# The inverse of the next head pair and half of its chain operands, made between the chunks of the present chain

## The chip, the cores and the metric

One Trainium2 chip, one core. The metric is the device time of one execution in microseconds, as the median of the runs; beside it stands one execution that the hardware profiler recorded, and every row below is from that one.

## The reference, cut to what matters

One block of a streaming encoder over 1024 tokens of width 1024. A combined projection feeds two groups: sparse attention, whose indexer picks the keys of every query, and RWKV-7 time mixing. Both results go through an output projection and then an MLP of width 4096.

```
step(state, inp):                      # RWKV-7, one token, 8 heads of 64
    r_t, w_t, k_t, v_t, kk_t, a_t = inp
    sa = einsum('bhij,bhj->bhi', state, -kk_t)
    state = (state * w_t[:, :, None, :] + sa[..., None] * (kk_t * a_t)[:, :, None, :]
             + v_t[..., None] * k_t[:, :, None, :])
    return state, einsum('bhij,bhj->bhi', state, r_t)
_, out = lax.scan(step, state0, xs)

h = RMSNorm(x) * (1 + sc1) + sh1 ;  proj = h @ w_in  ->  p_a (attention), p_b (RWKV)
x = x + gt1 * (concat(dsa_attention(p_a), rwkv7_time_mix(p_b)) @ w_out)
u = relu((RMSNorm(x) * (1 + sc2) + sh2) @ w_ff1) ;  x = x + gt2 * ((u * u) @ w_ff2)
```

## The kernel before, in words

The tokens are worked in two halves (hf 0 and 1) of 512. The order in which the code is written is: projections of half 0, RWKV of half 0, attention projections of half 0, indexer of half 0, RWKV projections of half 1, attention of half 0, RWKV of half 1, attention projections of half 1, output projection and MLP of half 0 (with indexer and attention of half 1 hung into it), MLP of half 1. A tile scheduler turns that order into one fixed queue for each engine: what is written earlier has priority, what is not ready by the scheduler's own reckoning lets later work go first. So the large projection matmuls (`dense`, tile ps_mm, with the operands hh, hl, whi, wlo) fill the places between the small matmuls of RWKV and of the indexer. Each engine then works its queue strictly in the written order.

RWKV runs over 4 pairs of heads (j = 0 to 3), and each pair over 8 chunks of 64 tokens:

- `rwkv_feat`: decays, keys and the lower-triangular products Lb and KR of a pair; it ends with BKs on POOL.
- `rwkv_feat2`: the other operands of the chain: Mt (the product `ps_c<-KR,wrec`, masked on DVE), the transposed values (`ps_c<-con,v`, copied by ACT into UV and Vbd) and BKn (`ps_c<-con,BKs`, copied by ACT).
- `rwkv_inv`: the inverse of the chunks' unit-triangular matrices, into TT: 15 pairs of a DVE multiplication (ytmp) and a DVE subtraction (Y), two DVE transposes (D, AT), then four groups of 32x32 matmuls, AT·Lc, D·Gs, AT·Lb, D·Gs, with an ACT copy or a DVE step between them.
- `rwkv_chain`: the recurrence. A chunk is `ps_o<-Vbd,Mt` and `ps_o<-H,KR` on PE, Xb on DVE, `ps_c<-Xb,TT` on PE, UV on DVE and Ub on ACT, `ps_c<-UV,BKn` and `ps_o<-Ub,Lb` on PE, the state H on DVE and On on ACT. The next chunk needs H.
- `rwkv_out`: the normalised output of a pair, written back to memory.

`rwkv` writes, for each j: feat2(j), the whole chain(j), out(j-1), the inverse of j+1, feat(j+2). PSUM has two buffers each for the tags mm, f and c and one each for dx and o; chain, feat2 and inverse all share the two buffers of c.

Of the kernel before, what the change touches and what calls it, by code (L numbers as in the profile page):

```python
# [111 lines left out]
def body(tc, I, out, dbg=None):  # L112
# [475 lines left out]

    def rwkv_feat2(hf, j, R, gp):
        mark('feat%d%d' % (hf, j))  # L590
        R["Mt"] = Mt = gp.tile([128, 8, 2, 64], F32, name="Mt", tag="Mt", bufs=1)
        R["BKn"] = BKn = gp.tile([128, 8, 128], F32, name="BKn", tag="BKn", bufs=1)
        R["UV"] = UV = gp.tile([128, 8, 128], F32, name="UV", tag="UV", bufs=1)
        gram(R["Kh"], R["KR"], Mt, "c")

        pn = pst("c")
        for c in range(4):
            T.transpose(pn[:, c * 128:c * 128 + 128], R["v2"][:, 2 * c:2 * c + 2, :].rearrange("p a b -> p (a b)"), ident)
        pn3 = pn.rearrange("p (a b) -> p a b", a=4)
        for e in range(2):  # L600
            q = slice(e * 64, e * 64 + 64)
            A.copy(UV[64:128].rearrange("p (a e) b -> p a e b", e=2)[:, :, e, :], pn3[q])
            for h in range(2):
                r = slice(h * 64, h * 64 + 64)
                A.copy(R["Vbd"][r].rearrange("p (a e) h b -> p a e h b", e=2)[:, :, e, h, :],
                       pn3[q, :, h * 64:h * 64 + 64])
        for u in (0, 4):
            pn = pst("c")
            for c in range(4):
                T.transpose(pn[:, c * 128:c * 128 + 128], flat(R["BKs"][:, u + c, :, :]), ident)  # L610
            A.copy(BKn[:, u:u + 4, :], pn.rearrange("p (a b) -> p a b", a=4))

    def rwkv_inv(hf, j, R, rp):
# [21 lines left out]
        for c in range(15, 0, -1):  # L635
            t0 = c // 4
# [5 lines left out]
            V.tensor_tensor(y, y, tv, ALU.subtract)  # L642
        D = rp.tile([128, 8, 32], F32, name="D", tag="D", bufs=1)
# [4 lines left out]
        pg, pf = pst("c"), pst("c")  # L648
# [18 lines left out]
        pg = pst("c")  # L667
# [9 lines left out]
        pf = pst("c")  # L677
# [9 lines left out]
    def rwkv_chain(hf, j, R, rp):  # L687
# [3 lines left out]
        On = rp.tile([128, 4, 2, 64], F32, name="On", tag="On", bufs=2)  # L691
        for c in range(8):
# [21 lines left out]
        return On  # L714
# [428 lines left out]
    def rwkv_head(hf, rp):  # L1143
# [182 lines left out]
```

## Time and profile before

| what | value |
|---|---|
| median of 3 runs | 1786.07 us (1786.06 to 1786.14) |
| the profiled execution | 1783.31 us, its span 1781.5 us, mean granted TensorE clock 0.971 |
| PE busy | 1613.9 us, 91% of the span |
| DVE, ACT, POOL busy | 1060.6, 871.5, 557.7 us |

A busy time is the union of an engine's recorded spans; idle time is the rest of the window. A row of the waits says which instruction ended an engine's idle time. The rows themselves stand in the section below.

### The profile page before, as it was taken

How to read it: one execution, taken by the hardware profiler on the slowest of the kernel's cores; microseconds unless marked ns; L12 is line 12 of the kernel's file. 1: busy time of each engine (PE TensorE's matmuls, PEld its weight loads, DVE VectorE, ACT ScalarE, POOL GpSimd, SP SyncE). 2: the span in 40 equal slices, each digit the busy share in tenths (PEclk: the TensorE clock that was granted, in tenths of full speed). 3: DMA queues.
4: the chain of work that ended last, by engine and by line, in shares of the span. 5: the costliest groups of instructions: out<-in, count | busy, mean ns of one | idle time of the engine just before them, and what ended most of it. 6: DMA issues, size and time to landing. Idle time of an engine off the chain costs nothing. (4 is left out here: it accounts for less than half of the span.)

```text
span 1781.5 us, 27231 instructions
## 1 busy us (share of the span) xinstructions
PE 1613.9 (91%) x9380; PEld 1208.7 (68%) x9380; DVE 1060.6 (60%) x2701; ACT 871.5 (49%) x1792; POOL 557.7 (31%) x751
## 2 busy tenths in 40 slices
PE   6997888998778888997968999999999999999998
PEld 3785656666555665674646666777886788888887
DVE  4777677639877777646999558863114233333333
ACT  3324454545547545435845864775235252525251
POOL 3556334443440243433224464113554300000000
PEclk9998999999899999998979999999999999999999
DMA  9885226234343543212112234324332433333332
GB/s 311 281 294 170 81 79 194 84 101 134 101 119 128 156 137 101 61 53 68 41 50 75 71 96 125 84 84 146 103 96 70 122 110 96 98 95 95 96 99 72
DMA packets 264016, 203.89 MB, mean 114 GB/s; under 512 B 17299, under 2 KB 218003, under 8 KB 263878
## 3 DMA queue, kind: packets, MB, share of 16 engines
q1 hardware_dynamic: 253122, 182.90, 34.2%
q10 hardware_dynamic: 10628, 19.24, 2.9%
q8 instruction: 74, 1.21, 0.3%
q14 instruction: 64, 0.52, 0.1%
q0 software_dynamic: 128, 0.01, 0.0%
HBM read 173.32 MB, written 28.78 MB: 113 GB/s over the span
## 5 line engine op out<-in xcount | busy, mean ns | idle before, releaser
L136 POOL TENSOR_TENSOR wlo<-wraw,whi 128x256 fp32r<-128x256 f32 x512 | 400.6, 805 | 658.1 <-ACT whi L394 589.9
L121 PE MATMUL ps_mm<-hh,whi 128*128 128x512 f32 (+1 forms) x1024 | 419.1, 410 | 22.1 <-DVE acca L930 4.1
L394 ACT CAST whi<-wraw 128x512 fp32r<-128x512 f32 x384 | 235.7, 616 | 408.3 <-PE ps_mm L121 378.0
L121 PE MATMUL ps_mm<-hl,whi 128*128 128x512 f32 (+1 forms) x1024 | 417.5, 408 | 2.8 <-DVE hl L384 1.8
L121 PE MATMUL ps_mm<-hh,wlo 128*128 128x512 f32 (+1 forms) x1024 | 418.2, 408 | 0.4
L121 PEld LDWEIGHTS ps_mm<-hh,whi 128*128 128x128 f32 (+1 forms) x1024 | 196.0, 192 | 68.8 <-issue 9.1
L121 PEld LDWEIGHTS ps_mm<-hh,wlo 128*128 128x128 f32 (+1 forms) x1024 | 196.2, 192 | 46.0 <-issue 7.4
L121 PEld LDWEIGHTS ps_mm<-hl,whi 128*128 128x128 f32 (+1 forms) x1024 | 196.3, 192 | 44.3 <-issue 4.8
L121 PE MATMUL ps_mm<-uh,whi 128*128 128x512 f32 x512 | 205.1, 401 | 17.3 <-ACT whi L394 5.7
L121 PE MATMUL ps_mm<-ul,whi 128*128 128x512 f32 x512 | 204.7, 400 | 6.0 <-DVE ul L1118 6.0
L121 PE MATMUL ps_mm<-uh,wlo 128*128 128x512 f32 x512 | 204.4, 399 | 0.8 <-POOL wlo L136 0.5
L396 DVE TENSOR_TENSOR wlo<-wraw,whi 128x512 fp32r<-128x512 f32 x128 | 88.2, 689 | 130.3 <-ACT whi L394 130.3
L915 ACT ACTIVATE jka<-sc,canda 128x1024 bf16<-128x1024 f32 (+1 forms) x93 | 90.1, 969 | 82.5 <-DVE canda L913 57.3
L121 PEld LDWEIGHTS ps_mm<-uh,whi 128*128 128x128 f32 x512 | 97.7, 191 | 44.0 <-ACT whi L394 8.6
L121 PEld LDWEIGHTS ps_mm<-ul,whi 128*128 128x128 f32 x512 | 97.7, 191 | 29.8 <-DVE ul L1118 8.3
L121 PEld LDWEIGHTS ps_mm<-uh,wlo 128*128 128x128 f32 x512 | 97.9, 191 | 24.7 <-POOL wlo L136 2.5
L1124 DVE SCALAR_TENSOR_TENSOR xT<-ps_mm,mod,xT 128x512 f32<-128x512 f32 x64 | 47.9, 748 | 110.7 <-PE ps_mm L121 110.6
L1118 DVE TENSOR_TENSOR ul<-ur,uh 128x512 fp32r<-128x512 f32 x64 | 44.3, 692 | 80.6 <-ACT uh L1117 80.5
L1023 DVE CUSTOM_DVE_ANT_0 L<-ps_f,mk 128x512 f32<-128x512 f32 (+3 forms) x96 | 51.8, 554 | 31.5 <-PE ps_f L121 16.4
L705 ACT COPY Ub<-ps_c 64x64 f32<-64x64 f32 x128 | 26.3, 206 | 72.8 <-DVE UV L703 68.7
L1029 ACT ACTIVATE L<-L,m 128x128 f32<-128x128 f32 (+7 forms) x64 | 49.6, 776 | 18.6 <-DVE m L1026 14.2
L1042 ACT COPY PT<-ps_c 128x512 f32<-128x512 f32 (+3 forms) x96 | 42.5, 479 | 28.8 <-PE ps_c L1041 25.8
(329 smaller groups left out, 2601.4 us busy)
## 6 DMA issues: line engine op xcount, KB each, us to landing
wraw<-in_w_ff_dram SPq DMA_DIRECT2D x256, 256.0 KB, 2.6
wraw<-in_w_in_dram SPq DMA_DIRECT2D x92, 256.0 KB, 3.3
mraw<-in_w_ada_dram SPq DMA_DIRECT2D x64, 256.0 KB, 4.6
mraw<-in_w_ada_dram SPq DMA_DIRECT2D x16, 512.0 KB, 10.7
wraw<-in_w_out_dram SPq DMA_DIRECT2D x32, 256.0 KB, 2.6
rkvd<-shy ACTq DMA_DIRECT2D x24, 256.0 KB
xin<-in_x_dram SPq DMA_DIRECT2D x8, 512.0 KB, 6.5
rt<-rnd SPq DMA_DIRECT2D x32, 128.0 KB, 3.1
```

Of the source, the lines that this page charges most:

```text
L121: r = T.matmul(out, lhsT, rhs, start=start, stop=stop, **kw)
L136: G.tensor_tensor(o[:, c], a[:, c], b[:, c], op)
L394: (A.copy if HE[GRP[0]] == "a" else V.tensor_copy)(hi[:, :, 0:M], raw[:, :, 0:M])
L396: (V if LE[GRP[0]] == "v" or LE[GRP[0]] == "m" and GRP[1] else InHalves).tensor_tensor(lo[:, :, 0:M], raw[:, :, 0:M], hi[:, :, 0:M].bitcas ...
L705: (V.tensor_copy if CE[2] == "v" else A.copy)(Ub[h * 64:h * 64 + 64, h, :], pu[u, h * 64:h * 64 + 64])
L915: A.activation(jka[:, 0:width(b)], sc[b], AF.Sign, scale=-1.0, bias=0.0 if bit == 31 else canda.bitcast(F32)[:, i:i + 1], accum_out=ca[:, ...
L1023: V.tensor_tensor_reduce(L[:, c0:c0 + n], ps[:, 0:n], masks[b][:, c0:c0 + n], 1.0, -3e38, ALU.add, ALU.max, m2[:, pc:pc + 1])
L1029: A.activation(L[:, 0:W], L[:, 0:W], AF.Exp, bias=m2[:, 2:3], accum_out=m2[:, 3:4])
L1042: (A.copy if ((pc + h) % 2 if PTE == 0 else h if PTE == 1 else PTE == 2) else V.tensor_copy)(pT[:, c0:c0 + n], px[:, 0:n])
L1118: V.tensor_tensor(b, r, a.bitcast(F32), ALU.subtract)
L1124: V.scalar_tensor_tensor(xT[:, d, :], ps, mod[:, 40 + d:41 + d], xT[:, d, :], ALU.mult, ALU.add)
```

## The change

`rwkv_inv` becomes a generator that stops before each of its 15 steps and before its transposes, takes PSUM of tag f where it took c, and orders each of its DVE multiplications behind the last H update that has been written. `rwkv_feat2` makes four chunks at a time (u = 0 or 4), with Mt, BKn and UV in tiles that stay for all pairs. `rwkv_chain` becomes a generator that stops after every chunk. `rwkv` then writes for each j: chunk 0, one step of the inverse of j+1, out(j-1); after each later chunk three more steps; after chunk 4 the first half of feat2(j+1); after chunk 7 the rest of the inverse, the second half of feat2(j+1) and feat(j+2). For pair 0 both halves of feat2 stand ahead of feat(1). No arithmetic is added or left out: the transposes of v, and the ACT copies of them, are made in two pieces each.

```diff
-    def rwkv_feat2(hf, j, R, gp):
+    def rwkv_feat2(hf, j, R, u):
-        gram(R["Kh"], R["KR"], Mt, "c")
+        gram(R["Kh"], R["KR"], R["Mt"], "c", (u,))
...
-    def rwkv_inv(hf, j, R, rp):
+    def rwkv_inv(hf, j, R, rp, tag="f"):
...
         for c in range(15, 0, -1):
+            yield
...
-            V.tensor_tensor(tv, L2[:, :, c * 32:c * 32 + c].unsqueeze(3).to_broadcast([128, 2, c, n]),
+            r = V.tensor_tensor(tv, L2[:, :, c * 32:c * 32 + c].unsqueeze(3).to_broadcast([128, 2, c, n]),
                             Y2[:, :, c * 8 + t0:c * 8 + 4].unsqueeze(2).to_broadcast([128, 2, c, n]), ALU.mult)
+            order(r, chained[0])
...
-        pg, pf = pst("c"), pst("c")
+        pg, pf = pst(tag), pst(tag)
...
-                V.scalar_tensor_tensor(H[r, h, :], H[r, h, :], WC[r, c:c + 1], ph[r, h * 64:h * 64 + 64],
-                                       ALU.mult, ALU.add)
+                chained[0] = V.scalar_tensor_tensor(H[r, h, :], H[r, h, :], WC[r, c:c + 1], ph[r, h * 64:h * 64 + 64],
+                                                    ALU.mult, ALU.add)
...
+        setup(0)
+        for u in (0, 4):
+            rwkv_feat2(hf, 0, R[0], u)
         R[1] = rwkv_feat(hf, 1, L4, rp, bp)
         for j in range(4):
...
-            rwkv_feat2(hf, j, R[j], bp)
-            On[j] = rwkv_chain(hf, j, R[j], bp)
-            for w in OR:
-                if w == "o" and j > 0:
-                    rwkv_out(hf, j - 1, R[j - 1], On[j - 1], sg, bp)
-                if w == "i" and j < 3:
-                    rwkv_inv(hf, j + 1, R[j + 1], rp)
-                if w == "f" and j < 2:
-                    R[j + 2] = rwkv_feat(hf, j + 2, L4, rp, bp)
+            for c in rwkv_chain(hf, j, R[j], On[j]):
+                for _ in range(1 if c == 0 else 3):
+                    next(inv, None)
+                if c == 0 and j > 0:
+                    rwkv_out(hf, j - 1, R[j - 1], On[j - 1], sg, bp)
+                if c == 4 and j < 3:
+                    rwkv_feat2(hf, j + 1, R[j + 1], 0)
+            for _ in inv:
+                pass
+            if j < 3:
+                rwkv_feat2(hf, j + 1, R[j + 1], 4)
+            if j < 2:
+                R[j + 2] = rwkv_feat(hf, j + 2, L4, rp, bp)
```

In PE's queue of the kernel before, this is what stands between the last matmul of chain 0 in half 0 and the first of chain 1 (`ps_o<-Vbd,Mt`); two stretches are left out between the pieces.

```order
L121 MATMUL ps_o<-Ub_1569,Lb 128x128
L121 MATMUL ps_c<-AT,Lc 32x32 x32
L121 MATMUL ps_f<-KR,Bh 64x128 x3
L121 MATMUL ps_c<-D,Gs 32x32 x32
L121 MATMUL ps_f<-KR,Bh 64x128 x5
...
L121 MATMUL ps_c<-AT,Lb 32x32 x16
...
L598 MATMUL ps_c<-con,v_1579 128x128 x4
L121 MATMUL ps_f<-w2a,tw 128x128 x3
L121 MATMUL ps_dx<-asq,con 128x512
L610 MATMUL ps_c<-con,BKs 128x128 x4
L121 MATMUL ps_o<-Vbd,Mt 128x128
```

In the changed kernel the same queue, from the same matmul of chain 0 to the first one of chain 1, has only the second half of feat2 and two products of the next feat.

```order
L121 MATMUL ps_o<-Ub_1569,Lb 128x128
L121 MATMUL ps_c<-KR,wrec 64x128 x8
L598 MATMUL ps_c<-con,v_1632 128x128 x2
L121 MATMUL ps_f<-w2a,tw 128x128 x4
L121 MATMUL ps_f<-xa,a2w 128x512
L609 MATMUL ps_c<-con,BKs 128x128 x4
L121 MATMUL ps_o<-Vbd,Mt 128x128
L121 MATMUL ps_o<-H_120,KR 128x128
```

The matmuls of the inverse have moved up, ahead of the last two chunks of chain 0: this is chunk 6 to chunk 7 of chain 0 in the changed kernel, where `ps_f<-AT,Lc` and `ps_f<-D,Gs` stand ahead of the chunk's own `ps_c<-UV,BKn` and `ps_c<-Xb,TT`.

```order
L121 MATMUL ps_c<-Xb_1567,TT_1310 128x128
L121 MATMUL ps_f<-AT,Lc 32x32 x14
L121 MATMUL ps_c<-UV,BKn 128x128
L121 MATMUL ps_f<-AT,Lc 32x32 x3
L121 MATMUL ps_o<-Ub_1569,Lb 128x128
L121 MATMUL ps_f<-AT,Lc 32x32 x15
L121 MATMUL ps_o<-Vbd,Mt 128x128
L121 MATMUL ps_o<-H_119,KR 128x128
L121 MATMUL ps_mm<-hl,whi 128x512
L121 MATMUL ps_f<-D,Gs 32x32 x32
L121 MATMUL ps_c<-Xb_1567,TT_1310 128x128
```

Counted in PE's queue, the number of ps_mm matmuls that stand ahead of a place is, before and after the change:

| place in PE's queue | before | after |
|---|---|---|
| half 0: first matmul of chain 0, 1, 2, 3 | 420, 481, 533, 615 | 385, 482, 518, 588 |
| half 0: last matmul (`ps_o<-Ub,Lb`) of chain 0, 1, 2, 3 | 476, 524, 599, 680 | 482, 518, 588, 640 |
| first and last score matmul (kiH, iqs) of the indexer of half 0 | 743, 787 | 694, 736 |
| first `ps_f<-w2a,tw` of half 1 | 944 | 944 |
| half 1: first matmul of chain 0 | 1103 | 1103 |
| half 1: last matmul of chain 3 | 1360 | 1354 |
| all | 4648 | 4648 |

## Rows read from the trace of the kernel before

**Rows 1.** From the profile's page: the span, the busy time of each engine, and the chain of work that ended last, by engine and by line.

```profile
span 1781.5 us, 27231 instructions
...
PE 1613.9 (91%) x9380; PEld 1208.7 (68%) x9380; DVE 1060.6 (60%) x2701; ACT 871.5 (49%) x1792; POOL 557.7 (31%) x751
...
PE 22%; DVE 1%; DMA 0%; ACT 0%; issue 0%; DVEq 0%; ACTq 0%
PE ps_mm L121 22%; DVE hv L382 0%; DVE hv L381 0%; DMA out_dram<-xout 0%; DVE hl L384 0%; PE ps_f L1083 0%; PE ps_dx L1083 0%; DVE xT L1124 0%; DVE ul L1118 0%; ACT xo L1084 0%; PE ps_dx L121 0%; DVE xout L1084 0%; ACT xout L1084 0%; ACTq L1084 0%; DVEq L381 0%
```

**Rows 2.** Busy time of each engine by stretch; the columns are the stretch, its length, then busy us of PE, PEld, DVE, ACT and POOL with the count of instructions, the granted clock, the DMA share and GB/s. The first begins where the head's features are under way; the next three begin at the first matmul of chain 0, 1 and 2 of half 0, the fifth at that of chain 3; 380 to 531 us is the output of pair 3, the attention projections and the indexer of half 0, and the first features of half 1; 620 to 797 us is RWKV of half 1; the last is the MLPs.

```profile
159.00:191.70 32.70, 26.58 (x335) 19.57 (x332) 23.77 (x58) 13.19 (x28) 15.43 (x25) 0.90 0.34 97
191.70:241.40 49.70, 44.41 (x438) 30.93 (x437) 32.39 (x94) 24.14 (x63) 21.16 (x33) 1.00 0.25 75
241.40:298.90 57.50, 50.22 (x444) 32.50 (x442) 42.73 (x138) 27.77 (x69) 19.46 (x28) 0.97 0.41 130
298.90:347.70 48.80, 44.43 (x443) 33.71 (x442) 34.09 (x111) 26.56 (x77) 22.34 (x30) 1.00 0.44 134
347.70:380.00 32.30, 31.89 (x160) 22.27 (x159) 16.70 (x51) 16.59 (x43) 13.65 (x18) 1.00 0.26 74
380.00:531.00 151.00, 120.40 (x647) 89.51 (x647) 122.16 (x426) 80.11 (x167) 66.27 (x91) 0.92 0.41 118
620.00:797.00 177.00, 160.06 (x1460) 114.27 (x1457) 116.86 (x333) 84.10 (x217) 68.37 (x98) 1.00 0.28 90
1100.00:1781.50 681.50, 669.49 (x3342) 534.30 (x3340) 266.32 (x514) 299.28 (x522) 108.90 (x147) 1.00 0.33 97
```

**Rows 3.** The waits of PE from 159 to 380 us: us in total, times, longest.

```profile
PE ps_f L121 <- DVE rk L547: 8.3, 3, 4.1
PE ps_c L121 <- DVE UV L703: 2.1, 3, 1.6
PE ps_c L121 <- DVE Xb L698: 1.8, 3, 1.0
PE ps_f L121 <- DVE Lb L585: 1.5, 1, 1.5
```

**Rows 4.** The waits of PE from 380 to 531 us, same columns.

```profile
PE ps_f L121 <- DVE acca L930: 8.4, 1, 8.4
PE ps_c L121 <- DVE AT L646: 5.3, 1, 5.3
PE ps_mm L121 <- DVE acca L930: 4.1, 2, 2.5
PE ps_dx L121 <- ACT asq L753: 3.3, 1, 3.3
```

**Rows 5.** The waits of PE from 620 to 797 us, same columns.

```profile
PE ps_c L121 <- DVE UV L703: 4.9, 8, 1.0
PE ps_c L121 <- DVE Xb L698: 2.3, 5, 0.9
...
PE ps_c L121 <- DVE Y L642: 1.1, 1, 1.1
```

**Rows 6.** PE's timeline in half 0: the state products of two neighbouring chunks of chain 0, then its last matmul, some of what stands behind it, and the first matmul of chain 1. Start, duration, engine, line, operation, count, and idle time before it.

```profile
209.55 0.39 PE L121 MATMUL ps_o<-H,KR 128*128 128x128 f32 x2
...
213.05 0.39 PE L121 MATMUL ps_o<-H,KR 128*128 128x128 f32 x2
...
226.53 0.49 PE L121 MATMUL ps_o<-Ub,Lb 128*128 128x128 f32 x2
...
231.55 0.39 PE L121 MATMUL ps_mm<-hh,whi 128*128 128x512 f32 x1
231.78 0.39 PE L121 MATMUL ps_mm<-hl,whi 128*128 128x512 f32 x1
...
235.94 1.14 PE L121 MATMUL ps_c<-KR,wrec 64*64 64x128 f32 x15
...
240.97 0.66 PE L610 MATMUL ps_c<-con,BKs 128*128 128x128 f32 x4 [0.26 <-DVE Mt L585]
241.46 0.39 PE L121 MATMUL ps_o<-Vbd,Mt 128*128 128x128 f32 x2
```

**Rows 7.** PE's timeline: the last score matmul of the indexer of half 0, and the first two steps of the features of half 1 (the product with w2a, and that with rk).

```profile
423.99 0.39 PE L121 MATMUL ps_f<-kiL,iqs 128*128 128x512 f32 x1
...
471.24 1.05 PE L121 MATMUL ps_f<-w2a,tw 65*128 65x128 f32 x8
...
487.06 1.22 PE L121 MATMUL ps_f<-rk,con 128*128 128x512 f32 x1 [8.44 <-DVE acca L930]
```

**Rows 8.** Groups of instructions from 159 to 800 us: the inverse's subtraction and multiplication on DVE, and the copies of the transposed values on ACT. Count, busy us, mean ns of one, idle time before them.

```profile
L642 DVE TENSOR_TENSOR Y<-Y,ytmp 128x24 f32<-128x24 f32 (+10 forms) x120 | 34.8, 290 | 3.1
L639 DVE TENSOR_TENSOR ytmp<-Lu,Y 128x24 f32<-128x24 f32 (+10 forms) x120 | 32.3, 269 | 3.0
...
L605 ACT COPY Vbd<-ps_c 64x256 f32<-64x256 f32 x32 | 11.8, 367 | 0.4
...
L602 ACT COPY UV<-ps_c 64x512 f32<-64x512 f32 x16 | 9.3, 580 | 13.4 <-PE ps_c L598 13.2
```

**Rows 9.** DVE's timeline in the first inverse: the same kind of multiplication twice.

```profile
164.25 0.19 DVE L639 TENSOR_TENSOR ytmp<-Lu,Y 128x28 f32<-128x28 f32 x1
...
165.65 0.73 DVE L639 TENSOR_TENSOR ytmp<-Lu,Y 128x44 f32<-128x44 f32 x1
```

More of the change, by code (lines that the diff above doesn't have):

```diff
@@ L574, in rwkv_feat, with gram @@
         return dict(KR=KR, Lb=Lb, WC=WC, bvs=bvs, Kh=Kh, BKs=BKs, v2=v2)
-    def gram(src, KR, dst, tag):
-        for u in (0, 4):
+    def gram(src, KR, dst, tag, us=(0, 4)):
+        for u in us:
             pz = pst(tag)
@@ L587, in gram @@
                             C("zmask").unsqueeze(1).to_broadcast([128, 4, 128]), ALU.mult)
-    def rwkv_feat2(hf, j, R, gp):
+    def rwkv_feat2(hf, j, R, u):
         mark('feat%d%d' % (hf, j))
-        R["Mt"] = Mt = gp.tile([128, 8, 2, 64], F32, name="Mt", tag="Mt", bufs=1)
-        R["BKn"] = BKn = gp.tile([128, 8, 128], F32, name="BKn", tag="BKn", bufs=1)
-        R["UV"] = UV = gp.tile([128, 8, 128], F32, name="UV", tag="UV", bufs=1)
-        gram(R["Kh"], R["KR"], Mt, "c")
+        BKn, UV = R["BKn"], R["UV"]
+        gram(R["Kh"], R["KR"], R["Mt"], "c", (u,))
+        pn = pst("c")
+        for c in range(2):
+            cc = u + 2 * c
+            T.transpose(pn[:, c * 128:c * 128 + 128], R["v2"][:, cc:cc + 2, :].rearrange("p a b -> p (a b)"), ident)
+        pn3 = pn[:, 0:256].rearrange("p (a b) -> p a b", a=2)
+        for e in range(2):
+            q = slice(e * 64, e * 64 + 64)
+            A.copy(UV[64:128, u:u + 4].rearrange("p (a e) b -> p a e b", e=2)[:, :, e, :], pn3[q])
+            for h in range(2):
+                r = slice(h * 64, h * 64 + 64)
+                A.copy(R["Vbd"][r, u:u + 4].rearrange("p (a e) h b -> p a e h b", e=2)[:, :, e, h, :],
+                       pn3[q, :, h * 64:h * 64 + 64])
@@ L596, in rwkv_feat2 @@
         pn = pst("c")
         for c in range(4):
[L598 to L611, printed above, removed]
-    def rwkv_inv(hf, j, R, rp):
+            T.transpose(pn[:, c * 128:c * 128 + 128], flat(R["BKs"][:, u + c, :, :]), ident)
+        A.copy(BKn[:, u:u + 4, :], pn.rearrange("p (a b) -> p a b", a=4))
+    def order(ins, other):
+        if other is not None:
+            tc.add_manual_dep(ins.ins, other.ins.name,
+                              mybir.DependencyInfo(mybir.DependencyClass.NoSync, mybir.DependencyReason.DATA), reason="order")
@@ L635, in rwkv_inv @@
         for c in range(15, 0, -1):
+            yield
+            mark('inv%d%d' % (hf, j))
             t0 = c // 4
@@ L666, in rwkv_inv @@
             (G.tensor_copy if qd % 2 else A.copy)(TT[r, :, o:o + 32], D[r])
-        pg = pst("c")
+        pg = pst(tag)
         Gs = rp.tile([128, 8, 32], F32, name="Gs", tag="Ld", bufs=1)
@@ L676, in rwkv_inv @@
             A.copy(Gs[r].rearrange("p a b -> p (a b)"), pg[r, 0:256])
-        pf = pst("c")
+        pf = pst(tag)
         for u in range(8):
@@ L685, in rwkv_inv, with rwkv_chain @@
             A.copy(TT[r, :, 32:64], pf[r, 0:256].rearrange("p (a b) -> p a b", b=32))
-    def rwkv_chain(hf, j, R, rp):
+    chained = [None]
+    def rwkv_chain(hf, j, R, On):
         mark('chain%d%d' % (hf, j))
@@ L709, in rwkv_chain @@
                 r = slice(h * 64, h * 64 + 64)
-                V.scalar_tensor_tensor(H[r, h, :], H[r, h, :], WC[r, c:c + 1], ph[r, h * 64:h * 64 + 64],
-                                       ALU.mult, ALU.add)
+                chained[0] = V.scalar_tensor_tensor(H[r, h, :], H[r, h, :], WC[r, c:c + 1], ph[r, h * 64:h * 64 + 64],
+                                                    ALU.mult, ALU.add)
             p = (c % 2) * 64
             A.copy(On[p:p + 64, c // 2, :, :].rearrange("p b c -> p (b c)"), px[64:128, 0:128])
-        return On
+            yield c
+            mark('chain%d%d' % (hf, j))
     def rwkv_out(hf, j, R, On, sg, rp):
@@ L1154, in rwkv_head @@
         R0["TT"] = TT0
-        rwkv_inv(hf, 0, R0, rp)
+        for _ in rwkv_inv(hf, 0, R0, rp):
+            pass
         return L4, R0
@@ L1166, in rwkv, with setup @@
             G.memset(t, 0.0)
+        kept = {n: bp.tile([128, 8, 128], F32, name=n) for n in ("Mt", "BKn", "UV")}
+        kept["Mt"] = kept["Mt"].rearrange("p a (b c) -> p a b c", b=2)
+        chained[0] = None
+        def setup(j):
+            R[j].update(kept, Vbd=Vbd, TT=TT[j % 2], Xb=Xb[j % 2], Ub=Ub[j % 2])
+        setup(0)
+        for u in (0, 4):
+            rwkv_feat2(hf, 0, R[0], u)
         R[1] = rwkv_feat(hf, 1, L4, rp, bp)
         for j in range(4):
-            R[j].update(Vbd=Vbd, TT=TT[j % 2], Xb=Xb[j % 2], Ub=Ub[j % 2])
+            inv = iter(())
             if j < 3:
-                R[j + 1]["TT"] = TT[(j + 1) % 2]
-            rwkv_feat2(hf, j, R[j], bp)
-            On[j] = rwkv_chain(hf, j, R[j], bp)
-            for w in OR:
-                if w == "o" and j > 0:
-                    rwkv_out(hf, j - 1, R[j - 1], On[j - 1], sg, bp)
-                if w == "i" and j < 3:
-                    rwkv_inv(hf, j + 1, R[j + 1], rp)
-                if w == "f" and j < 2:
-                    R[j + 2] = rwkv_feat(hf, j + 2, L4, rp, bp)
+                setup(j + 1)
+                inv = rwkv_inv(hf, j + 1, R[j + 1], rp)
+            On[j] = bp.tile([128, 4, 2, 64], F32, name="On", tag="On", bufs=2)
+            for c in rwkv_chain(hf, j, R[j], On[j]):
+                for _ in range(1 if c == 0 else 3):
+                    next(inv, None)
+                if c == 0 and j > 0:
+                    rwkv_out(hf, j - 1, R[j - 1], On[j - 1], sg, bp)
+                if c == 4 and j < 3:
+                    rwkv_feat2(hf, j + 1, R[j + 1], 0)
+            for _ in inv:
+                pass
+            if j < 3:
+                rwkv_feat2(hf, j + 1, R[j + 1], 4)
+            if j < 2:
+                R[j + 2] = rwkv_feat(hf, j + 2, L4, rp, bp)
         rwkv_out(hf, 3, R[3], On[3], sg, bp)
```

3 lines of the change are left out of this document (2 added, 1 removed).

## The prediction

> **What bounds the kernel now.** I read the page first: PE is busy for 1613.9 of 1781.5 us, and the chain that ended last is ps_mm matmuls on PE [rows 1]. So the time is PE's work plus PE's idle time, 167.6 us in all, and nothing in this change removes PE work. Next the busy time by stretch [rows 2] shows where that idle time lies. In the MLPs, from 1100 us, PE idles 12 of 681.5 us: a microsecond won earlier is neither won again nor lost there. RWKV of half 0 (159 to 380 us, the first five stretches) holds 221 − 197.5 = 23.5 us of idle time, the stretch behind it (380 to 531) 151 − 120.4 = 30.6, RWKV of half 1 (620 to 797) 177 − 160.1 = 16.9. In the stretch 380 to 531 DVE is busy 122 of 151 us, more than PE: there PE waits for DVE.
>
> The waits say what the idle time of half 0 is made of [rows 3]: the product with rk 8.3 us, three waits for UV 2.1, three for Xb 1.8, one for Lb 1.5. Behind RWKV they are long [rows 4]: 8.4 and 4.1 us for the top-k's acca, 5.3 for the inverse's AT, 3.3 for asq. In half 1 they are short again [rows 5].
>
> Then the seam between two chains, in PE's timeline [rows 6]. The last matmul of chain 0 starts at 226.53, the first of chain 1 at 241.46: 14.9 us in which no chunk runs, while a steady chunk takes 213.05 − 209.55 = 3.5 us. But PE works in that seam, on the inverse, on Lb and Mt of the next pair and on dense matmuls. The seam is latency of RWKV, not idle time of PE.
>
> **The change, part by part.** The terms follow from that: the time falls (a) by idle time of PE that goes, (b) by dense matmuls that leave RWKV of half 0 and later fall into places where PE would have waited for DVE anyway.
>
> Term (b). By the count in PE's queue, 680 dense matmuls stand ahead of the last matmul of chain 3 in half 0 before, 640 after. Back to back one takes 231.78 − 231.55 = 0.23 us [rows 6], so 40 × 0.23 = 9.3 us of PE work leave this stretch. (Which product of norm or output falls inside it differs too; I find under 1 us of net work in that and leave it out.) The inverse's matmuls, Mt, BKn and the transposes are only moved.
>
> Term (a), half 0. The new order gives chain 0 feat2 ahead of feat(1), so the head's waits (rk 4.1 and Lb 1.5 [rows 3]) come to stand beside feat2's matmuls: I take 3 of these 5.6 us as gone, between 0 and 5.6. The waits for Xb and UV (3.9 us) lie in first chunks, where DVE also ran the inverse. Now the inverse is cut into steps of one multiplication and one subtraction behind H: 0.27 + 0.29 = 0.56 us a step by the means [rows 8], three a chunk, 1.7 us. A chunk has 3.5 us, and while PE runs its products DVE is partly free, so I take 2 of the 3.9 us as gone, between −8 (a stall of a quarter microsecond in 32 chunks) and 3.9. The rest, rk's later 4.2 us, stays: feat(j+2) still starts at the seam, and its first products now stand close ahead of `ps_f<-rk`. Sum: 5 us of idle time gone, in half 0. With (b), RWKV of half 0 ends 14 to 15 us earlier; with both ends of (a) between 1.3 and 19.
>
> The smaller edits: ACT copies of the transposed values come in twice as many pieces. Before they cost 4 × 0.367 + 2 × 0.58 = 2.6 us a pair [rows 8]; after, between 2.6 (cost goes with width) and 5.3 (it doesn't). They now fall into chunks 4 to 6, where `ps_c<-Xb,TT` needs a buffer of c that they must leave. Dense matmuls stand around them in the queue, so I take nothing; without that cover it is up to 2.6 us a pair, 21 us for all eight, which would turn the forecast into a small loss and lies inside the range. The inverse in PSUM tag f instead of c removes its quarrel with Mt for two buffers and starts one with feat, whose products are written behind it: nothing either way. No DMA moves except feat(j+2)'s three loads and out(j−1)'s store, on SP, by a chunk or two.
>
> From 380 to 531 us. The indexer's first score matmul has 49 fewer dense matmuls ahead of it, its last one 51 fewer (787 to 736), yet the features of half 1 start behind the same 944. So 51 × 0.23 = 11.7 us of dense work now lie between the last score matmul (423.99) and `ps_f<-w2a` (471.24) [rows 7]. Can they be swallowed? The waits there are 8.4 + 4.1 us for acca [rows 4], 12.5 us: just enough. The top-k on DVE starts 14.5 us earlier and takes as long, so it ends 14.5 us earlier; PE comes to `ps_f<-rk` at 487.06 − 8.44 = 478.6 of work time before, and after at 478.6 − 14.5 + 11.7 − 4.1 = 471.7, while DVE is done at 487.06 − 14.5 = 472.6. Both limits meet, so about all of the 14.5 us are kept at the first chain of half 1, where both kernels stand at 1103 dense matmuls.
>
> Half 1. Both kernels have nearly the same dense work up to the end of chain 3 (1360 and 1354), so here only idle time counts: 16.9 us [rows 2], of which the waits for UV, Xb and Y are 8.3 [rows 5]. I take a gain of 4.5, from −5 to 8, and give back 6 × 0.23 = 1.4 us of dense work that comes later. From there on the queues are alike. Sum: 14.5 + 4.5 − 1.4 = 17.6, about 18 us. The profiled execution was 1783.31 us, 1.8 over its span and 2.8 under the median; I take the difference from the median: 1786.07 − 18 = 1768.
>
> **A rule that speaks against it.** In [rows 4] PE stood 5.3 us at AT·Lc, waiting for the DVE transpose AT, and everything behind it waited too. The Trainium skill, TensorE: Matmul & The Clock Gate, "Part 2: What happens when you issue a matmul", says that only weight loads are pulled ahead and that matmuls keep program order; that row agrees. The rule's result here is the third rival below.
>
> **The rivals.**
>
> *PE is the limit between the indexer and half 1.* The forecast needs the 11.7 us of deferred work to vanish into waits. If top-k finishes earlier than I think, or dense matmuls cut up by small ones take longer, PE is late at `ps_f<-rk`, and term (b) comes back. For it: both limits meet within 1 us. Against: 3.3 and 5.3 us more of waiting follow [rows 4]. With half of (b) lost and half 1 winning nothing: 14.5 − 5 − 1.4 = 8 us, 1778.
>
> *The change doesn't do what it says.* Idle time in the seam turns into idle time in the chunks: the Xb and UV waits grow by what the rk and Lb waits lose, and the deferred work comes back. For it: PE was busy in the seams, so a shorter seam alone is worth nothing. 1786, within 0.2% (3.6 us, about what a measurement of this kernel can tell from no change).
>
> *Slower: the inverse stops the chain.* AT·Lc and D·Gs now stand inside chunks 6 and 7, ahead of `ps_c<-UV,BKn` and `ps_c<-Xb,TT`. Where D or AT comes late, PE stops, and with it the recurrence. The steps on DVE may be late: while another engine worked beside it one multiplication took 0.73 instead of 0.19 us [rows 9], so three steps can cost 3 × 2 × 0.54 = 3.2 us more, nearly a chunk. There are six such inverses. It decides from 18 / 6 = 3 us of stall per inverse; at the 5.3 us of [rows 4] it is 32 us, so 32 − 18 = 14 slower, 1800; at 4 us each, 1792. Against: in the chunks before the last, dense matmuls stand ahead of each Xb product.
>
> **How the numbers follow.** The forecast has 0.52, PE as the limit 0.20, no change 0.11, slower 0.17. The forecast's own range is 1758 to 1776: both ends of half 0's idle term but for the stalls, and of half 1's. Faster by over 0.2% are the first two, less a little of the second: 0.71. Within 0.2%: 0.12. Slower: 0.17. A range that leaves out no more than 2 in 10 reaches from 1757, a little below which only the best ends of all terms together lie, over no change to 1790, part of the slower case.
>
> **What would show it.** Right: RWKV of half 0 (159 to the last matmul of chain 3) some 14 us shorter; seams of about 5 us instead of 14.9; chunks 5 to 7 not over 4.5 us; acca's wait of 8.4 us nearly gone; the first chain of half 1 some 14 us earlier; the MLPs as long as before. Wrong: a new wait of PE for AT, D or Gs inside the chains of more than 2 us, waits for UV and Xb above 15 us together, the granted clock of these stretches below the 0.90 to 1.00 of [rows 2], or a `ps_f<-rk` that starts with no wait before it and late.

## The result and the profile after

The changed kernel took 1806.74 us in the median (1802.89 to 1807.47), the kernel before 1786.11 beside it: a ratio of 1.0106, interval 1.0086 to 1.0125. It is slower by about 20 us, where 18 us of gain were forecast. Timed once more later it stood at 1.0076 (1.0047 to 1.0105). The median of the kernel before moved from 1786 to 1793 us over the experiments, so every kernel below is compared by its ratio to the kernel before timed beside it; three executions of 2197 to 8507 us, in a slow state of the chip, are left out. The rows are each of one execution: two of the changed kernel differ by 3.4 us at the end of half 0's RWKV (379.36 and 375.95), so differences of a few microseconds between rows of two kernels mean little.

The page of the changed kernel: span and busy times.

```profile
span 1801.1 us, 27326 instructions
...
PE 1622.8 (90%) x9380; PEld 1220.3 (68%) x9380; DVE 1049.7 (58%) x2701; ACT 876.5 (49%) x1840; POOL 562.1 (31%) x751
```

Against [rows 1] the span is 19.6 us longer. PE's busy time is 8.9 us longer for the same 9380 matmul records, and its idle time 178.3 instead of 167.6 us, 10.7 longer. So nearly half of the loss is not waiting: the recorded spans of the same matmuls cover more time.

Busy time by stretch, columns as in [rows 2]: half 0's RWKV, half 1's RWKV, and the last 681.5 us.

```profile
159.00:380.00 221.00, 190.78 (x1752) 132.46 (x1750) 146.01 (x443) 106.91 (x294) 89.33 (x126) 0.95 0.32 98
...
621.60:816.00 194.40, 170.04 (x1476) 123.69 (x1472) 112.24 (x334) 85.58 (x237) 71.49 (x101) 0.93 0.27 85
1119.60:1801.10 681.50, 670.64 (x3350) 535.61 (x3350) 265.30 (x511) 299.75 (x524) 114.07 (x149) 1.00 0.33 98
```

The last row is that of [rows 2] within 1.2 us of PE time: the MLPs play no part. In half 0 RWKV ends at 380 us as before. In half 1 it takes 194.4 us instead of the 175 or so of before, and the granted clock is 0.93 where [rows 2] had 1.00.

With the start of each chunk's first matmul read from PE's timeline, RWKV can be cut in three kinds of stretches:

| sum over both halves, us | before | after |
|---|---|---|
| six seams, last matmul of a chain to first of the next | 88.7 | 28.3 |
| chunk 0 to chunk 2, six chains (1 to 3 of each half) | 64.3 | 119.1 |
| chunk 2 to last matmul, all eight chains | 184.0 | 216.6 |

The change did what it says: the seams lost 60.4 us. Some of their work had to go into the later chunks (32.6 us). But the first two chunks of these six chains took 54.8 us more, although only out(j−1) and up to four steps of the inverse were written there. Seams and first two chunks together went from 153.0 to 147.4 us: what the seams lost came back there almost whole. Chain 0 of half 0 is not in the first two rows. Its first matmul now starts at 161.5 instead of 191.7 us, but its first chunk takes 25.3 us (6.7 before), and its last matmul starts at 225.61 instead of 226.53: that early start is worth nothing.

The waits of PE in half 0 and, behind that, in half 1, columns as in [rows 3].

```profile
PE ps_f L121 <- DVE rk L547: 7.0, 3, 3.3
PE ps_c L121 <- DVE Xb L710: 5.5, 11, 0.9
PE ps_c L121 <- DVE UV L715: 4.1, 5, 2.4
PE ps_f L121 <- DVE AT L656: 3.0, 1, 3.0
```

```profile
PE ps_f L121 <- DVE rk L547: 6.1, 2, 3.2
PE ps_c L121 <- DVE UV L715: 5.6, 3, 2.7
```

There are new waits for UV, at most 2.4 to 2.7 us long, and in half 1 waits for rk of 6.1 us, where the kernel before had 1.2. Xb and UV together come to 17.1 us in the two halves (half 1's Xb is 1.9), against 11.1 before: the prediction had named 15 as a sign that it is wrong. It had also warned of waits for AT inside the chains; there is one of 3.0 us in half 0 and none in the rows of half 1.

PE's timeline at the seam that [rows 6] showed: last matmul of chain 0, chunk 0 of chain 1, and the first matmuls of chunks 1 and 2.

```profile
225.61 0.49 PE L121 MATMUL ps_o<-Ub,Lb 128*128 128x128 f32 x2
...
229.51 0.39 PE L121 MATMUL ps_o<-Vbd,Mt 128*128 128x128 f32 x2
...
237.43 2.08 PE L121 MATMUL ps_f<-rk,con 128*128 128x512 f32 x2 [3.34 <-DVE rk L547]
239.29 1.92 PE L121 MATMUL ps_f<-con,sig 128*128 128x128 f32 x8
241.00 1.06 PE L744 MATMUL ps_c<-con,On 128*128 128x128 f32 x4
241.85 1.83 PE L121 MATMUL ps_c<-sg,g2w 128*128 128x512 f32 x2
243.53 0.39 PE L121 MATMUL ps_o<-Vbd,Mt 128*128 128x128 f32 x2
...
251.47 0.49 PE L121 MATMUL ps_c<-UV,BKn 128*128 128x128 f32 x2 [2.44 <-DVE UV L715]
...
253.78 0.63 PE L121 MATMUL ps_o<-Vbd,Mt 128*128 128x128 f32 x2
```

The seam is 229.51 − 225.61 = 3.9 us instead of 14.9. Then chunk 0 to chunk 1 takes 14.0 us (5.6 before), chunk 1 to chunk 2 another 10.3. PE waits 3.34 us at the product with rk and then runs slowly: that product's two records took 2.08 us and the next 512-column pair (sg, g2w) 1.83. The granted clock is 0.50 from 237.43 to 243.50 us, the lower of PE's two levels (1.2 and 2.4 GHz). Until chunk 1's first matmul at 243.53, PE works without a break on four products of the features and of the output (rk, sig, On, g2w) that stand ahead of it in its queue.

Why rk comes late, and what holds the rest of chunk 1, stands in DVE's timeline, from 232 to 251 us:

```profile
232.21 0.28 DVE L715 COPY UV<-ps_c 64x128 f32<-64x128 f32 x1 [0.44 <-PE ps_c L121]
236.18 1.20 DVE L547 SCALAR_TENSOR_TENSOR rk<-rT,prm,kp 128x512 f32<-128x512 f32 x1 [3.69 <-POOL kp L136]
237.30 0.56 DVE L722 SCALAR_TENSOR_TENSOR H<-H,WC,ps_c 64x64 f32<-64x64 f32 x2
...
249.33 0.69 DVE L750 TENSOR_TENSOR ob<-ob,ps_c 128x512 f32<-128x512 f32 x1 [1.25 <-POOL ob L136]
249.94 1.28 DVE L585 TENSOR_TENSOR Lb<-ps_f,conb 128x512 f32<-128x512 f32 x2
251.14 0.27 DVE L715 COPY UV<-ps_c 64x128 f32<-64x128 f32 x1
```

UV of chunk 0 starts at 232.21, but H of chunk 0 only at 237.30, 5.1 us later. Ahead of H in DVE's queue stands rk of pair 2, and DVE sat 3.69 us until POOL's kp came. Chunk 1 needs H, but H is not what it waited for last: H is done at 237.86, and chunk 1's first matmul starts 5.7 us later, when PE's queue comes to it. So the late kp stops both queues, and it is PE's, with the wait for rk and the half clock behind it, that sets the start of chunk 1. Later chunk 1's UV stands behind ob of the previous pair (waiting 1.25 us for POOL) and two masks of Lb. POOL's timeline says why kp is late:

```profile
231.85 1.67 POOL L184 TENSOR_TENSOR gst<-gst,mhalf 128x8 f32<-128x8 f32 x1 [1.17 <-DVE gst L739]
233.60 1.18 POOL L136 TENSOR_TENSOR On<-On,gst 128x256 f32<-128x256 f32 x2
234.74 1.40 POOL L136 TENSOR_TENSOR kp<-kp,kT 128x256 f32<-128x256 f32 x2
```

kp waits behind the normalisation of pair j−1's output, 1.67 us of gst and 1.18 of On, which the change wrote ahead of chain j's chunk 1 as well. The same picture stands at all four places where the features of pairs 2 and 3 are made: rk starts at 236.18, 294.06, 674.62 and 734.17 us after waits of 3.61 to 3.69 us for kp, and H follows 1.1 us behind each. From the end of H to the next chunk's first matmul it is 5.7, 5.5, 4.4 and 4.1 us there; in the kernel before it was at most 0.8 us after chunk 0 of the same chains.

Why there? In the kernel before, the features of pair 2 were made during chain 0, not behind it. These are their product with w2a, that with rk, and the first of those with Bh, in PE's timeline of the kernel before, half 0:

```profile
188.22 0.49 PE L121 MATMUL ps_f<-w2a,tw 65*128 65x128 f32 x2
...
201.55 0.70 PE L121 MATMUL ps_f<-rk,con 128*128 128x512 f32 x1 [1.72 <-DVE rk L547]
...
227.63 0.65 PE L121 MATMUL ps_f<-KR,Bh 64*64 64x128 f32 x6
```

From w2a to Bh they had 39 us, a whole chain, and DVE's waits for kp came to 3.0 us over all eight pairs. In the changed kernel the product with w2a starts at 227.32 us and those with Bh at 244.93: they begin one chain later and have 18 us, around chunk 0. By the count of ps_mm matmuls ahead of the product with w2a (order of PE's queue, pairs 2 and 3) it is 417 and 481 before and 482 and 518 after in half 0, and 1104 and 1168 before, 1176 and 1215 after in half 1. The features lost the lead of a chain.

### The profile page after: what moved, and what is told of

Read it like the earlier page. It is cut to its first block, busy times and chain, and to the rows that moved or that the text cites. A ratio compares the mean times of both kernels' runs of the same rounds, so it can differ in the third digit from the quotient of the medians.

```text
span 1801.1 us, 27326 instructions
## 1 busy us (share of the span) xinstructions
PE 1622.8 (90%) x9380; PEld 1220.3 (68%) x9380; DVE 1049.7 (58%) x2701; ACT 876.5 (49%) x1840; POOL 562.1 (31%) x751
## 5 line engine op out<-in xcount | busy, mean ns | idle before, releaser
L121 PE MATMUL ps_o<-PT,vj 128*64 128x128 f32 x576 | 50.6, 283 | 7.4 <-DMA vj<-vd 6.0
```

The source lines that it names most:

```text
L121: r = T.matmul(out, lhsT, rhs, start=start, stop=stop, **kw)
```

## The experiments

The first theory was: feat(j+2) and out(j−1) now stand in the queues in front of chunks 0 to 2, and nothing hides their latency there. Rival A: the inverse inside the last chunks costs. Rival B: the clock costs, whatever the waits.

**Later features.** The loop writes feat(j+1) after chunk 1 of chain j, and starts the inverse of that pair there:

```diff
             for c in rwkv_chain(hf, j, R[j], On[j]):
+                if c == 1 and 1 <= j < 3:
+                    R[j + 1] = rwkv_feat(hf, j + 1, L4, rp, bp)
+                    setup(j + 1)
+                    inv = rwkv_inv(hf, j + 1, R[j + 1], rp)
...
-            if j < 2:
-                R[j + 2] = rwkv_feat(hf, j + 2, L4, rp, bp)
```

> The changed kernel with feat(j+2) written after chunk 1 of chain j+1 instead of ahead of chain j+1; the inverse of that pair is then made after chunks 1 to 7. Theory: PE's wait for rk (3.3, 3.2 and 2.8 us in front of chunk 1, at half clock behind it) goes or becomes short, chunk 0 to chunk 1 of chains 1 and 2 falls from 11 to 14 us to 5 to 8, and the time to 1790 to 1798 us. Rival A (inverse in the last chunks): worse, since the inverse is squeezed into fewer chunks: 1806 to 1815. Rival B (clock): follows the clock.

Measured: 0.9961 (0.9936 to 0.9986), faster than the kernel before and 0.012 to 0.015 under the changed one. Chunk 0 to 2 of the six chains fell to 88.3 us; chunk 0 to 1 of chains 1 and 2 is 4.8, 10.1, 8.6 and 6.3 us. This speaks against Rival A: the inverse is squeezed into fewer chunks here, and the time is less.

**One chunk later and two** (`c == 2` with four steps of the inverse a chunk; `c == 3` with five):

> feat(j+2) one chunk later still, after chunk 2 of chain j+1, and four steps of the inverse after each chunk behind it; out(j-1) after chunk 0 as in the change. Theory: chunks 0 to 2 of chains 1 to 3 get shorter by 1 to 3 us each, but the inverse comes later and AT.Lc is waited for behind chunk 7; 0.993 to 1.000. Rival A (the inverse in the last chunks costs): 1.000 to 1.006, slower than with feat after chunk 1.

> feat(j+2) after chunk 3 and five steps of the inverse after each chunk behind it. Theory: the gain of later features is used up once their latency no longer stands in front of chunk 2, and the inverse then ends later: 0.993 to 0.998, no better than after chunk 2. If a chunk later still gains as from chunk 1 to chunk 2: 0.988 to 0.992.

Measured: 0.9935 (0.9908 to 0.9963) and 0.9942 (0.9920 to 0.9964). After chunk 2 is the lowest ratio of all kernels run, though its interval touches those of its neighbours. The windows of the kernel with features after chunk 2, for RWKV of the two halves:

```profile
159.00:365.50 206.50, 181.23 (x1732) 126.25 (x1731) 139.18 (x439) 104.46 (x288) 82.69 (x119) 0.98 0.33 102
605.60:786.30 180.70, 159.31 (x1425) 114.14 (x1425) 110.99 (x352) 84.34 (x234) 67.14 (x95) 0.95 0.29 91
```

Half 0's RWKV ends at 365.02 us, 13.7 us earlier than before (the forecast had said 14.5), half 1's takes 180.7 us, still longer than the 175 of before.

**Out later.** `if c == 0 and j > 0` becomes `if c == 3 and j > 0`:

> The changed kernel with out(j-1) written after chunk 3 of chain j instead of after chunk 0. Theory (the features of pair j+2 and the output of pair j-1 now stand in every queue between chunk 0 and chunk 2 of chain j, and stop the recurrence there): out's share goes away, its POOL power and product (1.67 + 1.18 us) ahead of kp, its transposes and the g2w product on PE (about 3 us), its ob on DVE ahead of UV. The stretch from chunk 0 to chunk 2 of chains 1 and 2 falls from 22 to 24 us to 16 to 19, the time to 1788 to 1797 us. Rival A (the inverse inside chunks 5 to 7 is what costs): no change, 1803 to 1809. Rival B (the lower granted clock is what costs, whatever the waits): the time follows the clock, so no change if the clock of RWKV of half 1 stays near 0.9.

Measured: 1.0064 (1.0044 to 1.0083), chunk 0 to 2 in sum 105.6 us: a part of the loss, less than expected; chunk 2 to the end rose to 233.4. POOL's timeline in this kernel shows that the edit did not move what it was meant to move:

```profile
232.10 1.67 POOL L184 TENSOR_TENSOR gst<-gst,mhalf 128x8 f32<-128x8 f32 x1 [1.17 <-DVE gst L739]
233.85 1.18 POOL L136 TENSOR_TENSOR On<-On,gst 128x256 f32<-128x256 f32 x2
234.99 1.40 POOL L136 TENSOR_TENSOR kp<-kp,kT 128x256 f32<-128x256 f32 x2
```

The scheduler still puts gst and On ahead of kp; only out's matmuls and ob went back.

**Both later**:

> feat(j+2) after chunk 1 of chain j+1 and out(j-1) after chunk 3. With feat moved, the longest wait of PE left in RWKV is that of out's transposes for POOL's On (6.6 us in half 0, 8.2 in half 1). Theory (features and output in front of the first chunks): that wait goes, out's POOL work no longer stands beside feat's; 4 to 10 us less than feat moved alone, ratio 0.990 to 0.995. Rival A (out's own latency doesn't matter once feat is away): the same as feat moved alone, 0.996 within 0.002.

Measured: 1.0007 (0.9987 to 1.0028), so worse than later features alone, which neither side expected. Chunk 0 to 2 fell to 75.2 us in sum, but chunk 2 to the end rose to 256.9 (232.9 with feat alone): out's work now falls on the chunks that hold the inverse, which may be why; no run shows it.

**The inverse in one piece behind the chain** (the two lines with `next(inv, None)` are left out):

> The changed kernel with the inverse not taken apart: it is written whole after chunk 7, feat2 in halves as in the changed kernel. Theory: chunk 0 to 2 stays at over 20 us, since feat(j+2) and out(j-1) stay where they are, and the seams get their 10 us back: 1806 to 1830 us. Rival A (the inverse inside the chain costs 33 us in chunks 2 to 7 of all chains): the time falls to 1785 to 1797.

Measured: 1.0149 (1.0122 to 1.0176). Its waits on PE from 221 to 400 us:

```profile
PE ps_f L121 <- DVE AT L656: 13.3, 2, 9.2
```

With the inverse behind the chain, its wait for AT is 13.3 us in two places. That refuses Rival A: in this kernel the inverse is better inside, by 0.004 to 0.007.

**The half of feat2 inside the chain**, priced by taking it out again (with feat after chunk 1):

> feat(j+2) after chunk 1 of chain j+1, but both halves of feat2(j+1) behind chunk 7, so that only the inverse lies inside the chain. This prices the half of feat2 inside the chain. Theory: each seam is longer by the first half of feat2 (about 2 to 3 us), six seams, but PE has dense work for it: ratio 0.996 to 1.002. Rival (the copies of feat2 on ACT in chunks 4 to 6, which hold the two PSUM buffers of c, cost up to 2.6 us a pair): faster than with the first half inside, 0.988 to 0.995.

Measured: 0.9989 (0.9971 to 1.0008); the seams grow from 15.6 to 33.4 us in sum. By the two ratios the half inside is worth 0.003, but their intervals overlap, so no gain is shown; that it costs up to 2.6 us a pair is refused.

**The PSUM tag** (`tag="f"` becomes `tag="c"`), in the change and with feat after chunk 2:

> The changed kernel with the inverse back in PSUM tag c, nothing else. In the prediction the tag was taken as worth nothing. If so: ratio 1.008 to 1.013, as the change. If the inverse in f is what stands in the way of feat's products with rk and sig: 1.000 to 1.006. If c makes it worse, since the chain's own products need c: above 1.014.

> feat(j+2) after chunk 2 and the inverse in PSUM tag c. If the tag and the place of feat are two separate costs, their gains add: 0.9935 less about a hundredth, 0.980 to 0.988. If both are two ways to take the same thing away (feat's products out of the way of chunks 0 to 2), the tag gives nothing more: 0.990 to 0.998, and c may then cost, since the chain uses it.

Measured: 0.9997 (0.9976 to 1.0017) and 1.0022 (1.0001 to 1.0043). In the change, one word takes the whole loss away; with later features it costs 0.009. The queue says what it does. With tag c the counts ahead of w2a are 420, 478, 1109 and 1174, those of the kernel before within 6; in PE's timeline the features of pair 2 begin in chain 0 again:

```profile
191.32 0.61 PE L121 MATMUL ps_f<-w2a,tw 65*128 65x128 f32 x4
...
200.46 1.13 PE L121 MATMUL ps_f<-rk,con 128*128 128x512 f32 x2 [1.03 <-DVE rk L547]
```

So the tag is what took the lead away. The reason lies in the writing order: the inverse in f is written ahead of feat(j+2), so the features' products come behind it in the use of the two f buffers. But c costs the chain, which uses it itself: from chunk 2 to the end all chains together take 241.8 us with c in the change and 240.2 with later features, 216.6 and 231.6 with f. With feat after chunk 2 and tag c the counts ahead of w2a are 420, 479, 1101 and 1169, so there the features move back to the early place and that edit is lost. With c in the change, rk of pair 3 still waits for kp, but H of chunk 0 has gone ahead of it on DVE. The row below is chunk 1's first matmul, in PE's timeline:

```profile
241.84 0.57 DVE L722 SCALAR_TENSOR_TENSOR H<-H,WC,ps_c 64x64 f32<-64x64 f32 x2 [0.57 <-PE ps_c L121]
246.16 1.20 DVE L547 SCALAR_TENSOR_TENSOR rk<-rT,prm,kp 128x512 f32<-128x512 f32 x1 [3.75 <-POOL kp L136]
```

```profile
247.00 0.64 PE L121 MATMUL ps_o<-Vbd,Mt 128*128 128x128 f32 x2
```

H is done at 242.41 and chunk 1 still starts 4.6 us later: PE stands 2.05 us at out's transposes, waiting for POOL's On, and works on them and on g2w. An early H alone does not give an early chunk.

**The wait filled.** Three products without use ahead of the one with rk:

```diff
+            pb = pst("f")
+            if j > 1:
+                for _ in range(3):
+                    mmul(pb, C("oblk"), at)
...
-        pb = pst("f")
```

> The changed kernel with three products without use (fp32, 128x512) written into PE's queue ahead of the product with rk, for pairs 2 and 3 of each half, in the waits of about 3 us there. Rival B (the granted clock that falls behind these waits is the cost; PE's busy time is 8.9 us longer than before with the same work): the clock stays up, the time falls by 4 to 9 us, to 1797 to 1803. Theory (the latency of the features stands in front of chunk 1): the wait is only filled, the time stays within 3 us of 1806 or rises by up to 4.

Measured: 1.0033 (1.0016 to 1.0050). More work on PE, and 0.004 to 0.007 faster than the change (clear of the change as first timed; the interval of the second timing just touches). PE's timeline at the same place:

```profile
234.22 2.84 PE L121 MATMUL ps_f<-at,con 128*128 128x512 f32 x6
237.92 1.12 PE L121 MATMUL ps_f<-rk,con 128*128 128x512 f32 x2 [0.86 <-DVE rk L551]
...
240.43 1.02 PE L121 MATMUL ps_c<-sg,g2w 128*128 128x512 f32 x2
```

PE's idle time ahead of rk is 0.86 instead of 3.34 us, and the two products behind take 1.12 and 1.02 us instead of 2.08 and 1.83. That is the clock at 2.4 GHz instead of 1.2: the granted clock from chunk 0 to chunk 2 is 0.95 here and 0.86 in the change. Over the whole execution PE is busy for 1626.3 us, 12.4 of them with the useless products, so the useful ones take 1613.9 us: as much as in the kernel before, and the 8.9 us that the change had added are gone. PE's idle time falls by 9.7 us, into which the useless products went. So Rival B is part of it: of a loss of 0.008 to 0.011, filling the waits gives back 0.004 to 0.007, by PE's clock. The chains do not get shorter by it: from the last matmul of the chain before, the four places take 67.2 us in sum to chunk 1 instead of 74.9, but 113.5 to chunk 2 instead of 113.7.

**Without the product with rk**:

> The changed kernel without the bonus product of pairs 2 and 3: r*k*r_k and its sum over a head (the product with rk) are left out there and bvs is a copy of the values, so that PE has nothing to wait for there. It takes away the one wait in front of chunk 1 (3.3, 3.2 and 2.8 us, at half clock behind it) and about 1.1 us of PE work a pair. Theory: the next wait, for KR and Bh ahead of chunk 1's UV, takes part of it; 8 to 14 us less than the change, ratio 1.002 to 1.006. Rival (the PSUM tag alone is the cost, whoever waits in it): the rk product frees a buffer of f too, so this doesn't tell it apart if it is faster; if it is not faster (1.008 to 1.013), the wait for rk was not the cost.

Measured: 1.0047 (1.0030 to 1.0064), the size expected, but the first chunks do not get shorter: chunk 0 to 2 stays at 122.2 us in sum. On DVE another instruction of the same features takes rk's place ahead of H:

```profile
239.26 0.69 DVE L570 SCALAR_TENSOR_TENSOR Bh<-at,wrec 128x512 f32<-128x512 f32 x1 [5.03 <-POOL at L136]
239.87 0.56 DVE L725 SCALAR_TENSOR_TENSOR H<-H,WC,ps_c 64x64 f32<-64x64 f32 x2
```

In PE's queue the product with Bh stands ahead of chunk 1 and waits for the same instruction:

```profile
240.01 3.44 PE L121 MATMUL ps_f<-KR,Bh 64*64 64x128 f32 x32 [4.47 <-DVE Bh L570]
...
244.73 0.39 PE L121 MATMUL ps_o<-Vbd,Mt 128*128 128x128 f32 x2
```

H now waits behind Bh, which waits for POOL, and so does PE. H is done at 240.43, 4.3 us ahead of chunk 1's first matmul. Read from DVE alone this points to DVE's order; by PE's rows it is PE's again that sets the chunk's start. Two runs were made on what of feat stands ahead of H.

**H ahead of rk** (feat one chunk later than in the change, `c == 0`), and **kp on DVE**:

```diff
-        EN(0).tensor_tensor(kp, kp, kT, ALU.mult)
+        (V if j > 1 else EN(0)).tensor_tensor(kp, kp, kT, ALU.mult)
```

> feat(j+2) written after chunk 0 of chain j+1, one chunk later than in the change. In DVE's queue H of chunk 0 now stands ahead of rk at all four places. Theory (H held behind rk, which waits for POOL's kp): nearly all of the gain of the later places comes with this one step, ratio 0.995 to 1.000, H of chunk 0 right behind its product. Rival (PE's order, with rk, sig and KR.Bh ahead of chunk 1 or 2): PE still meets them early, half of the gain at most, 1.001 to 1.006.

> The change with one operation on another engine: kp times kT of pairs 2 and 3 on DVE instead of POOL, so that rk no longer waits for POOL, whose queue has out(j-1)'s power and product ahead of it. feat stays where the change has it. Theory: rk starts some 2 to 3 us earlier at four places and H behind it, 8 to 12 us less, and the clock stays up there: ratio 0.999 to 1.004. Rival (PE's order): the KR, Bh and out products still stand ahead, 1.005 to 1.010.

Measured: 0.9951 (0.9934 to 0.9967) and 0.9956 (0.9940 to 0.9972), the first at the lower end of the theory's range, the second below it. DVE's timeline with feat after chunk 0: UV and H of chunk 0, then rk.

```profile
229.83 0.28 DVE L715 COPY UV<-ps_c 64x128 f32<-64x128 f32 x1 [0.60 <-PE ps_c L121]
231.13 0.58 DVE L722 SCALAR_TENSOR_TENSOR H<-H,WC,ps_c 64x64 f32<-64x64 f32 x2 [1.02 <-PE ps_c L121]
...
234.29 1.20 DVE L547 SCALAR_TENSOR_TENSOR rk<-rT,prm,kp 128x512 f32<-128x512 f32 x1 [0.27 <-POOL kp L136]
```

H starts 1.3 us behind UV. In PE's queue, too, chunk 1's first matmul (232.10 us) now stands ahead of the product with rk (235.54), so this run moves both queues at once. The features' work has gone one chunk on: chunk 0 to 1 takes 4.9, 5.0, 8.9 and 5.2 us at the four places, chunk 1 to 2 takes 18.2, 12.7, 9.4 and 14.7, and chunk 0 to 2 of the six chains is 106.1 us in sum. With kp on DVE, rk still stands ahead of H at this place, but hardly waits:

```profile
232.71 0.67 DVE L533 TENSOR_TENSOR kp<-kp,kT 128x512 f32<-128x512 f32 x1
233.47 0.75 DVE L547 SCALAR_TENSOR_TENSOR rk<-rT,prm,kp 128x512 f32<-128x512 f32 x1
234.14 0.57 DVE L722 SCALAR_TENSOR_TENSOR H<-H,WC,ps_c 64x64 f32<-64x64 f32 x2
```

and PE's timeline from chunk 0 to chunk 1 of chain 1 is

```profile
229.81 0.39 PE L121 MATMUL ps_o<-Vbd,Mt 128*128 128x128 f32 x2
...
234.91 1.02 PE L121 MATMUL ps_f<-rk,con 128*128 128x512 f32 x2
...
236.99 1.02 PE L121 MATMUL ps_c<-sg,g2w 128*128 128x512 f32 x2
237.85 0.38 PE L121 MATMUL ps_o<-Vbd,Mt 128*128 128x128 f32 x2
```

8.0 us instead of 14.0, at a granted clock of 1.00. About 3 us of that is PE's wait for rk, and 3 more the products behind it (6.1 us in the change, 2.9 here). Here feat, out, the inverse and the tag stand as in the change; the engine of one operation at four places moves the time by 0.012 to 0.015, from slower to faster than before. In the rows of the two executions the gain lies where it should: from the last matmul of the chain before to chunk 1 the four places take 11.9, 13.9, 13.5 and 17.0 us instead of 17.9, 19.2, 18.0 and 19.8, in sum 18.5 us less, and the spans differ by 17.9. The rival is not refused by this: it took PE's wait and its clock as given, and with an early kp both go, while the same products still stand ahead of chunk 1. H is done 3.1 us before chunk 1 begins here. So the late kp is shown to be the cost; that it acts through H on DVE is not. The edit also takes kp's 1.40 us out of POOL's queue, so what stands behind it there comes earlier; no run separates the two.

> feat(j+2) after chunk 2 and kp times kT of pairs 2 and 3 on DVE. Theory: where H no longer stands behind rk, the engine of kp is worth little: 0.991 to 0.996, as feat after chunk 2 alone. If the two add: 0.984 to 0.990.

Measured: 0.9950 (0.9930 to 0.9971): the two do not add, as is to be expected if both take the same wait away.

> The changed kernel itself, beside the same runs of the kernel before as these, since the cause is read from differences of under a hundredth: 1.0086 to 1.0125 as first timed.

Measured: 1.0076 (1.0047 to 1.0105), a little lower than first timed; the two intervals overlap.

## Why the prediction was wrong

The step that failed is in term (a): "The rest, rk's later 4.2 us, stays: feat(j+2) still starts at the seam, and its first products now stand close ahead of `ps_f<-rk`." The word "still" is wrong. The product with w2a that stands at the seam of [rows 6] before (237.01 us) belongs to pair 3; that of pair 2 had run at 188.22, a chain earlier. In the change it is pair 2's that starts at this seam (227.32 us). So the closeness to `ps_f<-rk` was seen and priced at nothing. What the runs show in its place: at four places rk waits 3.6 to 3.7 us for POOL's kp, PE waits 2.8 to 3.3 us for rk ahead of chunk 1, and what follows on PE runs at half the clock, wholly or in part.

The step behind it is "The inverse in PSUM tag f instead of c removes its quarrel with Mt for two buffers and starts one with feat, whose products are written behind it: nothing either way." The quarrel was named, but not that it would put feat a whole chain back: with tag c the loss of 0.008 to 0.011 is gone. The two costs are one, told from two sides. Its size by the rows is 18.5 us at the four places (the change against kp on DVE); by the ratios it is 0.0120 to 0.0150 of 1786, 21 to 27 us. That accounts for the loss of 20 us, but not for the whole way from the forecast: with kp on DVE the kernel is 8 us faster than before, and 18 were forecast. In its rows half 1's RWKV still takes 184.9 us, 174.9 before; why, no run shows.

By the other steps:

- Term (b), 40 dense matmuls that leave half 0's RWKV: right. From the last matmul of chain 3 to the first of half 1's chain 0 it is 242.1 us before and 242.3 after, with those 40 matmuls more in between: they cost nothing there. Had they stayed in half 0, it would probably have ended later still.
- RWKV of half 0 14.5 us shorter: it ended at the same time (378.69 us before and 379.36 after for the last matmul of chain 3). The head's wait for rk did fall, from 4.1 to 0.85 us. With features after chunk 2 half 0 is 13.7 us shorter, with kp on DVE 8.0.
- Half 1, 4.5 us of gain: 19.2 us of loss. Only 6 dense matmuls leave it, so there was little to cover the new waits; that this is the reason is not shown.
- The clock was in the text only as a sign of failure. Of the 19.6 us, 8.9 are PE's longer busy time, and filling the waits took them away.
- Where the copies of feat2 were taken as free, the rows agree: the waits for Vbd are under 1.5 us in a half, and moving the inner half of feat2 behind the chain gains nothing.
- The rival "slower" had the sign right and the mechanism wrong. It named the inverse as what stops the chain, at 1800 us. The inverse inside the chain is a gain: behind it, the ratio is 1.0149. The stop came from the features. It stands in two queues, since DVE works in order too, and H waited there behind rk. The Trainium skill, TensorE: Matmul & The Clock Gate, "Architectural detail", says that ACT and DVE are strictly first in, first out; the rows of DVE above agree, with 3.69 us of waiting at rk ahead of H.
- The forecast's own range, 1758 to 1776, does not follow from its terms: with the ends that the text gives (idle time of half 0 from 0 to 9.5 us, half 1 from −5 to 8) it would be 1761 to 1783. The result lies far outside either.

## What to carry to other kernels

Where a change gives a buffer tag a new user, look up where the old users of that tag now start: here the next-but-one pair's features lost a chain's lead without a line of theirs being edited. Then follow what moved on every in-order queue that the recurrence also uses, PE as well as DVE, and see in the rows which of them reaches the next step last: here H was ready 4 to 6 us before PE came to the chunk that needs it. Once the recurrence stands behind an instruction that waits for a third engine, the cure can be small: write that instruction later, or take the wait away. And price a wait on PE together with the clock behind it.

## What the runs showed of the hardware

Useless matmuls made a kernel faster: with 24 more matmul records in four waits of about 3 us, the ratio fell from between 1.0076 and 1.0106 to 1.0033. At the first of these places the granted clock behind the wait was 0.50 in the change and 1.00 with the wait filled, and the two 512-column pairs there took 2.08 and 1.83 us, then 1.12 and 1.02.
